# A four-layer mixer trunk on one core: z tiles as the first projections of attention and of gated DeltaNet, a longer lead for them, and the DeltaNet gates as 64 columns

## The chip, the core and the metric

The kernel runs on one core of one Trainium2 chip. The metric is the device time of one execution in microseconds (us). Three executions of the kernel before took 2756.51, 2757.06 and 2751.56 us, with a median of 2756.51. A further execution was recorded by the profiler: it took 2752.67 us, of which the profile's span (first to last instruction) is 2751.0 us, at a mean granted TensorE clock of 0.993. Engines are named as in the profile: PE is TensorE's matmul, PEld its load of the stationary operand, DVE is VectorE, ACT is ScalarE, POOL is GpSimd, SP is SyncE, which starts most transfers.

## The reference

Four layers work on x of 1024 tokens by 1024 features in float32: HGRN2, sliding-window attention (SWA), gated DeltaNet (GDN), HGRN2 again. Each layer does

```
h = rmsnorm(x) * (1 + scale) + shift        # shift, scale, gate come from the condition c (adaLN)
y = mixer(h)                                # ends with  (o * silu(z)) @ w_out
x = x + gate * y
```

What matters here is the combined input projection of the two layers in the middle.

```
# SWA: 16 query heads, 4 key/value heads of 64 features, window 128
q, k, v, z = split(h @ w_in, [1024, 1280, 1536])
q, k = rope(rmsnorm(q)), rope(rmsnorm(k))
o = banded softmax attention with a sink;   y = (o * silu(z)) @ w_out

# GDN: 8 query/key heads, 16 value heads of 128 features
qkv, z, a, b = split(h @ w_in, [4096, 6144, 6160])
q, k, v = split(silu(causal_conv(qkv)));  q, k = l2norm(q), l2norm(k)
beta = sigmoid(b);  g = -exp(a_log) * softplus(a + dt_bias)     # 16 heads each: 32 columns in all
o = gated delta rule over chunks;         y = (rmsnorm(o) * silu(z)) @ w_out
```

## The kernel before

**Precision and tiles.** h is kept transposed (features on the 128 partitions) in two halves of 512 tokens, each as a rounded part and the rest (`hhi[hf]`, `hlo[hf]`). Weights are split in the same way when they are loaded: `load_w` (L158 to L179) transfers 256 KB (`w_raw`), casts it on ACT (`w_hi`, L171) and subtracts on DVE (`w_lo`, L172). There are three buffers of `w_raw` and four each of `w_hi` and `w_lo`. A product takes three matmuls, hi by hi (L196), hi by lo (L197) and lo by hi (L198), all in `mm3`. A tile of `proj_fm` has 128 output features by 512 tokens: 8 steps of K by 3, that is 24 matmuls of 512 moving columns, with two loads of weights for each group of 128 features. A tile of `proj_tm` (SWA's q, k, v) has tokens on the partitions: two blocks of 128 tokens by 256 features, 48 matmuls of 256 columns (`projt_ps`), with four loads of weights for two tiles in a half. All of them draw from three PSUM buffers (`proj_ps`, two in most of the GDN layer), as do the tiles of the output projection (`out_ps`).

**Order.** The program is written in order of emission, and each instruction has a priority from a counter. A scheduler puts the instructions of each engine in a fixed order by these priorities and by what is ready. `high_priority(offset)` takes the given number off the priority of what is emitted inside it. `early(g)` emits the first projections of a layer with `offset=EO`, 60, and the loads of their weights with a further `EW`, 150. `burst()` uses 4000. `weave` mixes several streams of one layer by their stated lengths.

**From layer to layer.** The output projection and the norm run in halves of tokens. Half 0's norm is done while half 1 is still projected. After half 1's last output tile the norm of half 1 is emitted: `norm_stats` (L444 to L468) squares and sums x (L457, L458), gets the row sums by matmuls (`n_ps`, L461), takes an inverse root in small steps on DVE (L151 to L155) and spreads it by a matmul (`n_rb`, L468); `norm_apply` (L471 to L481) writes 8 slices of `n_t` (L479, DVE), `hhi` (L480, ACT) and `hlo` (L481, DVE). Its buffers are a pool that is closed behind it (`self.nst.close()`), and then the next layer opens its own pool and calls `early` with projections of half 0, which need nothing of half 1's norm.

**What early takes.** In SWA it is `kv(0)`: two tiles of k, then two of v. The eviction of k, `ev_k` (L1225 to L1242), is long: sum of squares, inverse root, rotary products (`rotate`, L1215 to L1218), four transposes (`kt_ps`), copies. That of v is one ACT copy (L1247). Behind it come the write of x's half 1 to memory (`spill_x`), `kv(1)`, and `proj(0, ds[0])`: q of group 0 in both halves, then its z. The eviction of z, `ev_z`, is a tanh on ACT (L1267) and one DVE operation (L1270). Then the groups follow, attention of one beside the projections of the next. In GDN it is `proj_kq(0, ds[0], ((0,),))`: one tile of k, one of q and two of z, all of half 0 of head pair 0. k and q go through `conv` (L603 to L619): a copy (L611), a scaled copy (L615), three DVE operations (L617), tanh (L618), a product (L619), over three `gd_tb` and two `gd_xs` buffers, and then transposes (L625). z takes a tanh (L693), one DVE operation (L695) into a single buffer `gd_zs`, and a transfer to memory (`od`). Then come `decays()`, the tiles of k and q of half 1, and the first `inverse` (first matmul `kk_ps`, L714), beside k and q of pair 1 and v and z of pair 0. After that the eight stages run, each with one pair's `scan`, the next pair's `inverse`, and projections as filling; the list `ZL` says which z tiles (pair, halves) fill which stage. In HGRN2 `early` takes q and f of half 0 and the beginning of v.

**decays()** computes the gates a and b (32 columns) for all tokens: for each half one `ab_ps` tile of 24 matmuls with 32 stationary columns (`gd_wab`: hi and lo of the gate weights, cast at L528 and subtracted at L529), a copy to `gd_abT` (L547), eight transposes (`abt_ps`, L550), and then a chain of some 30 small operations up to `d_ps` (L582), on which the first inverse waits.

Of the kernel before, what the change touches and what calls it, by code (L numbers as in the profile page):

```python
# [32 lines left out]
SB = {"q": 2, "tmp": 4, "qhi": 2, "pth": 2, "sm": 2, "zs": 2, "of": 3}  # L33


EO, EW = 60, 150
PRH, PRS, PR = 150, 200, (150, 150)

SPH, SPS = 0.2, 0.4
# [5 lines left out]
ADA_ORDER = (2, 0, 3, 1, 4, 5)  # L45
AO = ((2, True), (0, True), 0, D, (3, True), (1, True))

ZL = ((1, 0, 1), (2, 0, 1)), ((3, 0, 1),), ((4, 0, 1),), ((5, 0),), ((5, 1),), ((6, 0, 1),), ((7, 0, 1),), ()


def drain(g):
    for _ in g:
        pass
# [31 lines left out]
class Trunk:  # L85
# [423 lines left out]
    def gdn(self, i, side):  # L509
# [11 lines left out]
            return gp.tile([P, n], F32, name="gd_" + name, tag="gd_" + name, bufs=bufs)  # L521


        wv = gp.tile([P, 4, KT, 32], F32R, name="gd_wab", tag="blk", bufs=1)
        wab = [wv[:, 0], wv[:, 1]]
        raw = self.wp.tile([P, HT], F32, name="w_raw", tag="raw", bufs=RAW)[:, :KT * 32].rearrange("p (k n) -> p k n", k=KT)
        nc.sync.dma_start(raw, w_in[:, :, 6144:6176])
        nc.scalar.copy(wab[0], raw)  # L528
        nc.vector.tensor_tensor(wab[1], raw, wab[0].bitcast(F32), ALU.subtract)  # L529
        cw = self.taps  # L530

        cmask = gp.tile([P, P], F32, name="gd_cmask")
# [6 lines left out]

        def decays():  # L540
            ab = tl("tmp")
            abT = gp.tile([P, T], F32, name="gd_abT", tag="blk", bufs=1)[:32]
            for hf in range(2):
                ps = self.proj_ps("ab_ps")
                for k in range(KT):
                    self.mm3(ps[:32, :], (wab[0][:, k, :], wab[1][:, k, :]), (self.hhi[hf][:, k, :], self.hlo[hf][:, k, :]), k == 0, k == KT - 1)
                nc.scalar.copy(abT[:, hf * HT:(hf + 1) * HT], ps[:32, :])  # L547
            pt = self.psum("tr", "abt_ps", 1)
            for c in range(C):
                nc.tensor.transpose(pt[:, c * 32:(c + 1) * 32], abT[:, c * P:(c + 1) * P], self.ident[:32, :32])  # L550
            pab = pt[:, :256].rearrange("p (c n) -> p n c", c=C)
            hc = lambda x: x.rearrange("p (h c) -> p h c", h=H)
            par = tl("tmp")
            tri = par[:, P:2 * P]
            nc.gpsimd.memset(tri, 1.0)
            nc.gpsimd.affine_select(out=tri, in_=tri, compare_op=ALU.is_ge, fill=0.0, base=0, pattern=[[1, P]], channel_multiplier=-1)
            nc.sync.dma_start(par[:, 0:16], ins["gd_a_log"].to_broadcast([P, H]))
            nc.sync.dma_start(par[:, 16:32], ins["gd_dt_bias"].to_broadcast([P, H]))
            nc.scalar.activation(par[:, 0:16], par[:, 0:16], AF.Exp)
            nc.scalar.activation(hc(beta), pab[:, 16:32, :], AF.Exp, scale=-1.0)  # L560
            nc.vector.tensor_scalar(beta, beta, 1.0, None, ALU.add)
            nc.vector.reciprocal(beta, beta)
            x, e, s, s2, g = (ab[:, n * P:(n + 1) * P] for n in (0, 1, 2, 3, 0))
            nc.vector.tensor_tensor(hc(x), pab[:, 0:16, :], par[:, 16:32, None].to_broadcast([P, H, C]), ALU.add)

            nc.vector.scalar_tensor_tensor(e, x, -1.0, x, ALU.mult, ALU.max)
            nc.scalar.activation(e, e, AF.Exp, scale=-1.0)
            nc.vector.tensor_scalar(s, e, 2.0, None, ALU.add)
            nc.vector.reciprocal(s, s)
            nc.vector.tensor_tensor(s, s, e, ALU.mult)  # L570
            nc.vector.tensor_tensor(s2, s, s, ALU.mult)
            nc.vector.tensor_scalar(e, s2, 2.0 / 17, 2.0 / 15, ALU.mult, ALU.add)
            for n in (13, 11, 9, 7, 5, 3, 1):
                nc.vector.tensor_tensor(e, e, s2, ALU.mult)
                nc.vector.tensor_scalar(e, e, 2.0 / n, None, ALU.add)
            nc.vector.tensor_tensor(e, e, s, ALU.mult)
            nc.vector.tensor_scalar(x, x, 0.0, None, ALU.max)
            nc.vector.tensor_tensor(e, e, x, ALU.add)
            nc.vector.tensor_scalar(e, e, -1.0, None, ALU.mult)
            nc.vector.tensor_tensor(hc(g), hc(e), par[:, 0:16, None].to_broadcast([P, H, C]), ALU.mult)  # L580
            pd = self.psum("lev", "d_ps", 2)
            nc.tensor.matmul(pd[:, 0:P], tri, g, start=True, stop=True)  # L582
            nc.tensor.matmul(pd[:, P:2 * P], self.ones, g, start=True, stop=True)
            nc.vector.tensor_scalar(nd, pd[:, 0:P], -1.0, None, ALU.mult)
            nc.scalar.activation(ed, pd[:, 0:P], AF.Exp)
            nc.vector.tensor_scalar(ned, ed, -1.0, None, ALU.mult)
            nc.scalar.activation(edl, pd[:, P:2 * P], AF.Exp)
            nc.vector.tensor_tensor(wl, pd[:, P:2 * P], nd, ALU.add)
            nc.scalar.activation(wl, wl, AF.Exp)
            pt = self.psum("tr", "dt_ps", 1)  # L590
            nc.tensor.transpose(pt[:, :P], nd, self.ident)
            dT = tl("tmp")
            nc.vector.tensor_scalar(dT[:, :P], pt[:, :P], -1.0, None, ALU.mult)
            nc.sync.dma_start(ddr.rearrange("h (c t) -> (h c) t", t=P), dT[:, :P])
# [39 lines left out]
        def proj_kq(u, dd, halves=((0, 1),)):  # L634
# [18 lines left out]
            for hv in halves:  # L653
                yield from self.proj_fm(w_in, D + u * P, ev_k, hv)
                yield from self.proj_fm(w_in, u * P, ev_q, hv)
                if hv == (0,):
                    yield from proj_z(u, dd, hv)
                    return
            t8 = lambda name, n=C: gp.tile([P, n], F32, name="gd_" + name, tag=name, bufs=2 if name in ("r2", "gn") else 3)
            ms = dd["ms"]  # L660
# [225 lines left out]

        w_out, od, on = ins["gd_out_w"][0], self.od[1], self.par[:, 74:75]
        ds = [dict() for _ in range(U)]
        self.early(proj_kq(0, ds[0], ((0,),)))
        self.spill_x(1)  # L890
        decays()
        drain(proj_kq(0, ds[0], ((1,),)))
# [282 lines left out]
    def swa(self, i, side):  # L1175
# [70 lines left out]
            p3 = ps.rearrange("p (t n) -> p t n", t=2)  # L1246
            nc.scalar.copy(v[:, v2, :], p3)  # L1247

        def proj(g, d):
            d.update(q=[None, None], zs=[None, None], rq=[None, None])  # L1250

            def ev_q(tp, ps):
                hf = tp // 2
# [7 lines left out]
                    d["rq"][hf] = self.rsqrt(d["ms"], 16, "q", sp)  # L1261

            yield from self.proj_tm(self.load_tm(w_in, g * 256), ev_q)
            for m in range(2):
                def ev_z(hf, ps):
                    th = tl("tmp")
                    nc.scalar.activation(th, ps, AF.Tanh, scale=0.5)  # L1267
                    if m == 0:
                        d["zs"][hf] = tl("zs", n=2 * HT).rearrange("p (m t) -> p m t", m=2)
                    nc.vector.scalar_tensor_tensor(d["zs"][hf][:, m, :], th, 1.0, ps, ALU.add, ALU.mult)  # L1270

                c0 = 1536 + g * 256 + m * P
                yield from self.proj_fm(w_in, c0, ev_z)

        def mix(g, d, halves=(0, 1)):
            vg = v[:, :, g * 64:(g + 1) * 64]
# [68 lines left out]
                yield 1  # L1345

        def kv(hf):
            for c0, ev in ((1024, ev_k), (1280, ev_v)):
                yield from self.proj_tm(self.load_tm(w_in, c0), ev, (2 * hf, 2 * hf + 1))

        self.early(kv(0))
        self.spill_x(1)
        drain(kv(1))
        ds = [dict() for _ in range(G)]
        drain(proj(0, ds[0]))
        w_out, od = ins["sw_out_w"][0], self.od[0]
        for g in range(G - 1):
            weave(self.tc, (mix(g, ds[g]), 28000, 0, 1, PRS), (proj(g + 1, ds[g + 1]), 42000, 0, 1, 0), (take(side, NS[1]), NS[1], 0, 1, 0))
# [89 lines left out]
```

## Time and profile before

| | before |
|---|---|
| median of three runs | 2756.51 us (2751.56 to 2757.06) |
| the profiled execution | 2752.67 us |
| its span | 2751.0 us |
| PE busy | 2669.9 us, 97% |
| DVE busy | 2001.3 us, 73% |
| ACT busy | 1224.1 us, 44% |
| SWA: last output tile of the layer before, first attention work | 632 us, 712 us |
| GDN: last output tile of the layer before, first inverse | 1123 us, 1187 us |
| last HGRN2: last output tile of the layer before | 2175 us |

How to read it: a row of the profile gives line, engine, operation, the tiles it writes and reads, and a count, then busy time and the mean of one in ns, then the time its engine stood idle before it and what ended that. "projt_ps <- DVE w_lo L172: 5.8, 4, 2.9" in a list of waits says that PE, ahead of matmuls into `projt_ps`, stood idle for 5.8 us in all, 4 times, at most 2.9 us, and that DVE's write of `w_lo` ended it. In a timeline the first two columns are start and length in us. In a table of windows the columns are the window, its length, the busy time of PE, PEld, DVE, ACT and POOL with the number of instructions, the granted clock of TensorE (1.00 is full), the mean share of the 16 DMA engines that were busy, and GB/s. Matmuls overlap one another, so their durations don't add up: their pace is read from one start to the next.

### The profile page before, as it was taken

How to read it: one execution, taken by the hardware profiler on the slowest of the kernel's cores; microseconds unless marked ns; L12 is line 12 of the kernel's file. 1: busy time of each engine (PE TensorE's matmuls, PEld its weight loads, DVE VectorE, ACT ScalarE, POOL GpSimd, SP SyncE). 2: the span in 40 equal slices, each digit the busy share in tenths (PEclk: the TensorE clock that was granted, in tenths of full speed). 3: DMA queues.
4: the chain of work that ended last, by engine and by line, in shares of the span. 5: the costliest groups of instructions: out<-in, count | busy, mean ns of one | idle time of the engine just before them, and what ended most of it. 6: DMA issues, size and time to landing. Idle time of an engine off the chain costs nothing.

```text
span 2751.0 us, 51716 instructions
## 1 busy us (share of the span) xinstructions
PE 2669.9 (97%) x19217; PEld 2147.2 (78%) x19217; DVE 2001.3 (73%) x5669; ACT 1224.1 (44%) x3107; POOL 133.8 (5%) x352
## 2 busy tenths in 40 slices
PE   8999999998999999899999999999999999999999
PEld 4878888778878767677788877787778888887877
DVE  6685765778677778677898798988875757556575
ACT  4332333444445565444546455555543433333342
POOL 0000100000000000001101001100000000000000
PEclk9999999999999999999999999999999999999999
DMA  6232222344223243324343343432463211111133
GB/s 237 82 103 82 66 85 74 118 129 146 62 85 97 77 149 91 116 74 111 94 127 101 92 123 101 116 104 77 150 188 119 81 54 40 51 46 49 46 120 112
DMA packets 347666, 273.30 MB, mean 99 GB/s; under 512 B 68963, under 2 KB 276246, under 8 KB 347414
## 3 DMA queue, kind: packets, MB, share of 16 engines
q1 hardware_dynamic: 347126, 268.95, 32.8%
q8 instruction: 151, 2.47, 0.4%
q14 instruction: 101, 0.83, 0.1%
q0 software_dynamic: 288, 1.05, 0.1%
HBM read 224.77 MB, written 45.15 MB: 98 GB/s over the span
## 4 chain that ended last, share of the span: by engine, by line
PE 76%; DVE 11%; DMA 6%; ACT 4%; issue 2%; SPq 1%; POOL 0%; DVEq 0%; ACTq 0%
PE proj_ps L196 10%; PE proj_ps L198 10%; PE proj_ps L197 10%; PE outp_ps L198 4%; PE outp_ps L196 4%; PE outp_ps L197 4%; PE projt_ps L197 3%; PE projt_ps L198 3%; PE projt_ps L196 3%; DMA ada_w<-in_ada_w_dram 2%; PE lev_ps L1004 2%; DVE gd_tb L617 1%; PE pv_ps L1330 1%; DVE w_lo L172 1%; PE w_ps L859 1%
## 5 line engine op out<-in xcount | busy, mean ns | idle before, releaser
L196 PE MATMUL proj_ps<-hhi,w_hi 128*128 128x512 f32 x1664 | 686.1, 412 | 11.2 <-ACT gd_tb L615 8.6
L197 PE MATMUL proj_ps<-hlo,w_hi 128*128 128x512 f32 x1664 | 675.5, 406 | 0.0
L198 PE MATMUL proj_ps<-hhi,w_lo 128*128 128x512 f32 x1664 | 674.0, 405 | 0.0
L196 PEld LDWEIGHTS proj_ps<-hhi,w_hi 128*128 128x128 f32 x1664 | 315.5, 190 | 68.3 <-ACT gd_tb L615 11.0
L198 PEld LDWEIGHTS proj_ps<-hhi,w_lo 128*128 128x128 f32 x1664 | 314.9, 189 | 59.1 <-issue 1.2
L197 PEld LDWEIGHTS proj_ps<-hlo,w_hi 128*128 128x128 f32 x1664 | 315.3, 190 | 53.0 <-issue 1.4
L172 DVE TENSOR_TENSOR w_lo<-w_raw,w_hi 128x512 fp32r<-128x512 f32 x332 | 223.1, 675 | 168.2 <-ACT w_hi L171 165.6
L171 ACT CAST w_hi<-w_raw 128x512 fp32r<-128x512 f32 x332 | 201.9, 611 | 307.8 <-PE proj_ps L197 183.1
L197 PE MATMUL projt_ps<-w_lo,hhi 128*128 128x256 f32 x896 | 256.1, 290 | 5.8 <-DVE w_lo L172 5.8
L196 PE MATMUL projt_ps<-w_hi,hhi 128*128 128x256 f32 x896 | 256.1, 291 | 0.5 <-ACT w_hi L171 0.5
L198 PE MATMUL projt_ps<-w_hi,hlo 128*128 128x256 f32 x896 | 255.4, 290 | 0.0
L196 PE MATMUL outp_ps<-o_hi,w_hi 128*128 128x512 f32 x576 | 229.3, 400 | 2.9 <-ACT o_hi L1156 1.9
L198 PE MATMUL outp_ps<-o_hi,w_lo 128*128 128x512 f32 x576 | 228.0, 398 | 1.4 <-DVE w_lo L175 1.4
L197 PE MATMUL outp_ps<-o_lo,w_hi 128*128 128x512 f32 x576 | 228.8, 398 | 0.2
L197 PEld LDWEIGHTS projt_ps<-w_lo,hhi 128*128 128x128 f32 x896 | 170.7, 192 | 9.2 <-DVE w_lo L172 6.8
L196 PEld LDWEIGHTS projt_ps<-w_hi,hhi 128*128 128x128 f32 x896 | 170.5, 192 | 3.8 <-issue 1.2
L198 PEld LDWEIGHTS projt_ps<-w_hi,hlo 128*128 128x128 f32 x896 | 170.6, 192 | 2.3 <-issue 1.4
L617 DVE SCALAR_TENSOR_TENSOR gd_tb<-gd_xs,taps,gd_tb 128x512 f32<-128x512 f32 x192 | 144.2, 751 | 25.1 <-ACT gd_tb L615 21.5
L174 ACT ACTIVATE w_hi<-w_raw,par 128x512 fp32r<-128x512 f32 (+1 forms) x136 | 94.7, 698 | 142.9 <-PE outp_ps L197 98.8
L196 PEld LDWEIGHTS outp_ps<-o_hi,w_hi 128*128 128x128 f32 x576 | 108.6, 189 | 27.0 <-ACT o_hi L1156 3.9
L175 DVE SCALAR_TENSOR_TENSOR w_lo<-w_raw,par,w_hi 128x512 fp32r<-128x512 f32 (+1 forms) x136 | 96.8, 716 | 42.8 <-ACT w_hi L174 41.5
L198 PEld LDWEIGHTS outp_ps<-o_hi,w_lo 128*128 128x128 f32 x576 | 108.6, 189 | 24.2 <-DVE w_lo L175 1.9
(388 smaller groups left out, 4918.5 us busy)
## 6 DMA issues: line engine op xcount, KB each, us to landing
ada_w<-in_ada_w_dram SPq DMA_DIRECT2D x160, 256.0 KB, 2.8
w_raw<-in_hg_in_w_dram SPq DMA_DIRECT2D x136, 256.0 KB, 2.8
w_raw<-in_gd_in_w_dram SPq DMA_DIRECT2D x108, 256.0 KB, 3.1
o_in<-od SPq DMA_DIRECT2D x72, 256.0 KB, 3.3
w_raw<-in_gd_out_w_dram SPq DMA_DIRECT2D x64, 256.0 KB, 2.8
w_raw<-in_sw_in_w_dram SPq DMA_DIRECT2D x48, 256.0 KB, 3.0
w_raw<-in_hg_out_w_dram SPq DMA_DIRECT2D x40, 256.0 KB, 2.9
ada_w<-in_ada_w_dram SPq DMA_DIRECT2D x8, 1024.0 KB, 10.0
```

Source lines behind the costliest of these rows:

```text
L171: nc.scalar.copy(hi, raw)
L172: nc.vector.tensor_tensor(lo, raw, hi.bitcast(F32), ALU.subtract)
L174: nc.scalar.activation(hi, raw, AF.Copy, scale=scale)
L175: nc.vector.scalar_tensor_tensor(lo, raw, scale, hi.bitcast(F32), ALU.mult, ALU.subtract)
L196: mm(out, a[0], b[0], start=start, stop=False)
L197: mm(out, a[0], b[1], start=False, stop=False)
L198: mm(out, a[1], b[0], start=False, stop=stop)
L617: nc.vector.scalar_tensor_tensor(y, xs[:, j:j + HT], w(j), y, ALU.mult, ALU.add)
L859: nc.tensor.matmul(po[:, hd[a]], dd["u"][a, hf][:, cs], rhs, start=True, stop=True)
L1004: nc.tensor.matmul(pl[gs, c * 48:(c + 1) * 48], kg[:, c * P + g * 32:c * P + (g + 1) * 32], x[:, 4 * c + g, :], start=True, stop=True)
L1330: nc.tensor.matmul(po[a * 64:(a + 1) * 64], vg[:, n + 1 - nkb + b, :], p4[:, :, a, :], start=b == 0, stop=b == nkb - 1)
```

## The change

There are four parts.

1. `EO` goes from 60 to 200, for the `early` block of all four layers.
2. In SWA, `early` takes the two z tiles of half 0 of group 0, then v, then k of half 0. `kv` has v ahead of k in both halves. After `kv(1)` come q (both halves) and z of half 1 alone. The z weights of group 0 are loaded twice, four loads more.
3. In GDN, `early` takes four z tiles of half 0 (pairs 0 and 1), then k and q of half 0 of pair 0. `ZL` has z of pair 1 only for half 1 in the first stage. The z weights of pair 1 are loaded twice, four loads more.
4. In `decays()` the hi and lo weights of the gates stand side by side as 64 stationary columns, so that one matmul makes both products: per half 16 matmuls in place of 24, in a `burst`. The product lo by lo, which the three matmuls leave out, is included. The transposes have 64 columns, and a copy (ACT) and a sum (DVE) of 128x256 put the two parts together.

```diff
-EO, EW = 60, 150
+EO, EW = 200, 150
...
-ZL = ((1, 0, 1), (2, 0, 1)), ((3, 0, 1),), ((4, 0, 1),), ((5, 0),), ((5, 1),), ((6, 0, 1),), ((7, 0, 1),), ()
+ZL = ((1, 1), (2, 0, 1)), ((3, 0, 1),), ((4, 0, 1),), ((5, 0),), ((5, 1),), ((6, 0, 1),), ((7, 0, 1),), ()
...
-        wv = gp.tile([P, 4, KT, 32], F32R, name="gd_wab", tag="blk", bufs=1)
-        wab = [wv[:, 0], wv[:, 1]]
+        wab = gp.tile([P, 2 * KT, 64], F32R, name="gd_wab", tag="blk", bufs=1)[:, :KT, :]
...
-        nc.scalar.copy(wab[0], raw)
-        nc.vector.tensor_tensor(wab[1], raw, wab[0].bitcast(F32), ALU.subtract)
+        nc.scalar.copy(wab[:, :, 0:32], raw)
+        nc.vector.tensor_tensor(wab[:, :, 32:64], raw, wab[:, :, 0:32].bitcast(F32), ALU.subtract)
...
-                ps = self.proj_ps("ab_ps")
-                for k in range(KT):
-                    self.mm3(ps[:32, :], (wab[0][:, k, :], wab[1][:, k, :]), (self.hhi[hf][:, k, :], self.hlo[hf][:, k, :]), k == 0, k == KT - 1)
-                nc.scalar.copy(abT[:, hf * HT:(hf + 1) * HT], ps[:32, :])
+                ps = self.proj_ps("ab_ps")[:64]
+                with self.burst():
+                    for k in range(KT):
+                        nc.tensor.matmul(ps, wab[:, k, :], self.hhi[hf][:, k, :], start=k == 0, stop=False)
+                        nc.tensor.matmul(ps, wab[:, k, :], self.hlo[hf][:, k, :], start=False, stop=k == KT - 1)
+                nc.scalar.copy(abT[:, hf * HT:(hf + 1) * HT], ps)
...
-                nc.tensor.transpose(pt[:, c * 32:(c + 1) * 32], abT[:, c * P:(c + 1) * P], self.ident[:32, :32])
-            pab = pt[:, :256].rearrange("p (c n) -> p n c", c=C)
+                nc.tensor.transpose(pt[:, c * 64:(c + 1) * 64], abT[:, c * P:(c + 1) * P], self.ident[:64, :64])
...
+            p4, ab2 = pt.rearrange("p (c b n) -> p b c n", c=C, b=2), par[:, 2 * P:].rearrange("p (c n) -> p c n", c=C)
+            nc.scalar.copy(ab2, p4[:, 1])
+            nc.vector.tensor_tensor(ab2, ab2, p4[:, 0], ALU.add)
+            pab = ab2.rearrange("p c n -> p n c")
...
                 if hv == (0,):
-                    yield from proj_z(u, dd, hv)
                     return
...
-        self.early(proj_kq(0, ds[0], ((0,),)))
+        self.early(chain(proj_z(0, ds[0], (0,)), proj_z(1, ds[1], (0,)), proj_kq(0, ds[0], ((0,),))))
...
-            for c0, ev in ((1024, ev_k), (1280, ev_v)):
+            for c0, ev in ((1280, ev_v), (1024, ev_k)):
...
-        self.early(kv(0))
+        ds = [dict(q=[None, None], zs=[None, None], rq=[None, None]) for _ in range(G)]
+        self.early(chain(proj_z(0, ds[0], (0,)), kv(0)))
         self.spill_x(1)
         drain(kv(1))
-        ds = [dict() for _ in range(G)]
-        drain(proj(0, ds[0]))
+        drain(chain(proj_q(0, ds[0]), proj_z(0, ds[0], (1,))))
```

`proj_q` and `proj_z` of SWA are the two halves of the former `proj`, which now chains them.

More of the change, by code (lines that the diff above doesn't have):

```diff
@@ L541, in decays @@
             ab = tl("tmp")
-            abT = gp.tile([P, T], F32, name="gd_abT", tag="blk", bufs=1)[:32]
+            abT = gp.tile([P, T], F32, name="gd_abT", tag="blk", bufs=1)[:64]
             for hf in range(2):
-                ps = self.proj_ps("ab_ps")
-                for k in range(KT):
-                    self.mm3(ps[:32, :], (wab[0][:, k, :], wab[1][:, k, :]), (self.hhi[hf][:, k, :], self.hlo[hf][:, k, :]), k == 0, k == KT - 1)
-                nc.scalar.copy(abT[:, hf * HT:(hf + 1) * HT], ps[:32, :])
+                ps = self.proj_ps("ab_ps")[:64]
[4 more added lines that the diff above has]
+                nc.scalar.copy(abT[:, hf * HT:(hf + 1) * HT], ps)
             pt = self.psum("tr", "abt_ps", 1)
             for c in range(C):
-                nc.tensor.transpose(pt[:, c * 32:(c + 1) * 32], abT[:, c * P:(c + 1) * P], self.ident[:32, :32])
-            pab = pt[:, :256].rearrange("p (c n) -> p n c", c=C)
+                nc.tensor.transpose(pt[:, c * 64:(c + 1) * 64], abT[:, c * P:(c + 1) * P], self.ident[:64, :64])
             hc = lambda x: x.rearrange("p (h c) -> p h c", h=H)
             par = tl("tmp")
+            p4, ab2 = pt.rearrange("p (c b n) -> p b c n", c=C, b=2), par[:, 2 * P:].rearrange("p (c n) -> p c n", c=C)
+            nc.scalar.copy(ab2, p4[:, 1])
+            nc.vector.tensor_tensor(ab2, ab2, p4[:, 0], ALU.add)
+            pab = ab2.rearrange("p c n -> p n c")
             tri = par[:, P:2 * P]
@@ L1247, in ev_v, with proj_q @@
             nc.scalar.copy(v[:, v2, :], p3)
-        def proj(g, d):
-            d.update(q=[None, None], zs=[None, None], rq=[None, None])
+        def proj_q(g, d):
             def ev_q(tp, ps):
@@ L1263, in proj, with proj_z @@
             yield from self.proj_tm(self.load_tm(w_in, g * 256), ev_q)
+        def proj_z(g, d, halves=(0, 1)):
             for m in range(2):
@@ L1272, in proj @@
                 c0 = 1536 + g * 256 + m * P
-                yield from self.proj_fm(w_in, c0, ev_z)
+                yield from self.proj_fm(w_in, c0, ev_z, halves)
+        def proj(g, d):
+            return chain(proj_q(g, d), proj_z(g, d))
         def mix(g, d, halves=(0, 1)):
```

## The prediction

> **What bounds the kernel now.** I read the page first, then the waits of PE, then a table of windows at the places that the change touches, then the timeline of PE, ACT and DVE there, and last the tiles of the gate projection.
>
> ```profile
> span 2751.0 us, 51716 instructions
> PE 2669.9 (97%) x19217; PEld 2147.2 (78%) x19217; DVE 2001.3 (73%) x5669; ACT 1224.1 (44%) x3107; POOL 133.8 (5%) x352
> PE   8999999998999999899999999999999999999999
> PE 76%; DVE 11%; DMA 6%; ACT 4%; issue 2%; SPq 1%; POOL 0%; DVEq 0%; ACTq 0%
> ```
>
> The kernel is bound by TensorE: it is busy 2669.9 us of 2751.0, so all its idle time is 81.1 us. A quarter of the chain is other engines, though, and the slices show where to look: of 68.8 us each, only the first, the tenth (619 to 688 us) and the seventeenth (1100 to 1169) fall to 8. Only two things can shorten the time: fewer or cheaper matmuls, or less of those 81 us. Which waits they are, from the waits of PE (in total, times, longest):
>
> ```profile
> PE proj_ps L196 <- ACT gd_tb L615: 8.6, 4, 5.9
> PE projt_ps L197 <- DVE w_lo L172: 5.8, 4, 2.9
> PE ab_ps L196 <- DVE gd_zs L695: 1.3, 1, 1.3
> ```
>
> The first is in the GDN layer, the second in the SWA layer, each right after the projections that run ahead of the norm of half 1. Windows there and in the stages behind (us, busy time of PE, PEld, DVE, ACT, POOL, granted clock, DMA share, GB/s):
>
> ```profile
> 632.00:660.50 28.50, 27.78 (x220) 26.45 (x218) 26.34 (x67) 14.39 (x25) 0.00 (x0) 1.00 0.48 165
> 660.50:666.10 5.60, 1.31 (x10) 0.89 (x8) 3.73 (x7) 2.45 (x4) 0.00 (x0) 0.84 0.67 226
> 666.10:671.00 4.90, 4.85 (x22) 4.86 (x23) 4.43 (x14) 0.26 (x1) 0.00 (x0) 0.50 1.04 369
> 1148.50:1153.30 4.80, 4.65 (x14) 3.38 (x15) 3.39 (x6) 1.61 (x4) 2.06 (x10) 0.59 0.43 109
> 1198.00:1256.00 58.00, 50.16 (x236) 39.64 (x236) 50.22 (x147) 32.51 (x99) 4.25 (x10) 0.99 0.29 75
> 1380.00:1480.00 100.00, 99.90 (x698) 82.10 (x697) 85.64 (x253) 54.39 (x173) 7.81 (x20) 1.00 0.40 110
> 2176.00:2230.00 54.00, 53.73 (x438) 46.63 (x437) 35.21 (x88) 23.23 (x39) 1.53 (x4) 1.00 0.21 60
> ```
>
> In SWA, PE works without a break to 660.5, stands still for most of 5.6 us, and then has only half its clock for 4.9 us, so the stall costs about 2.4 us more than its length. The same happens in GDN after its 5.9 us. The steady GDN stage (1380 on) is at 99.9%, so time saved ahead of it is kept, and so is time lost. The last HGRN2 layer's start has 0.27 us idle in 54: nothing to gain there.
>
> **SWA: tiles of z first, v before k, and a lead of 200.** The cause of the stall stands on DVE's and PE's timelines:
>
> ```profile
> 655.03 0.68 DVE L1215 TENSOR_TENSOR sw_tmp<-projt_ps,sw_sm 128x512 f32<-128x512 f32 x1
> 664.74 0.75 DVE L481 SCALAR_TENSOR_TENSOR hlo<-n_t,mod,hhi 128x512 fp32r<-128x512 f32 x1 [1.87 <-ACT hhi L480]
> 665.41 1.28 DVE L172 TENSOR_TENSOR w_lo<-w_raw,w_hi 128x512 fp32r<-128x512 f32 x2
> ```
> ```profile
> 632.21 0.40 PE L198 MATMUL out_ps<-hg_ohi,w_lo 128*128 128x512 f32 x1
> 632.45 0.28 PE L196 MATMUL projt_ps<-w_hi,hhi 128*128 128x256 f32 x1
> ...
> 658.55 0.28 PE L198 MATMUL projt_ps<-w_hi,hlo 128*128 128x256 f32 x1
> 658.67 0.28 PE L196 MATMUL projt_ps<-w_hi,hhi 128*128 128x256 f32 x1
> 662.26 0.39 PE L197 MATMUL projt_ps<-w_lo,hhi 128*128 128x256 f32 x1 [1.43 <-DVE w_lo L172]
> 666.15 0.58 PE L197 MATMUL projt_ps<-w_lo,hhi 128*128 128x256 f32 x1 [2.91 <-DVE w_lo L172]
> ...
> 1139.72 0.39 PE L196 MATMUL proj_ps<-hhi,w_hi 128*128 128x512 f32 x1
> 1142.21 0.39 PE L198 MATMUL proj_ps<-hhi,w_lo 128*128 128x512 f32 x1
> ```
>
> PE wants the weights of k of half 1, and their low part waits on DVE behind the norm's last write of half 1. DVE had been busy 26.34 of 28.5 us with the norm, the weights and k's rotary eviction (L1215 is one of its operations) at once. How much of DVE that eviction took up to the norm's end, by its tiles sw_tmp and k_ms (windows of those alone), and what a load of weights and an eviction of z take there:
>
> ```profile
> 632.00:665.50 33.50, 1.20 (x8) 0.79 (x8) 4.94 (x8) 1.18 (x2) 0.98 0.50 171
> ```
> ```profile
> 632.00:665.50 33.50, 2.56 (x10) 0.98 0.50 171
> ```
> ```profile
> L172 DVE TENSOR_TENSOR w_lo<-w_raw,w_hi 128x512 fp32r<-128x512 f32 x332 | 223.1, 675 | 168.2 <-ACT w_hi L171 165.6
> ```
> ```profile
> L1270 DVE SCALAR_TENSOR_TENSOR sw_zs<-sw_tmp,proj_ps x16: 657/680/689, 732.3 to 996.1; 128x512 f32<-128x512 f32 x16
> ```
>
> The work on half 0 that needs no norm grows. A projt matmul starts 0.12 us after the last (658.55, 658.67), so the four tiles of 48 are 23 us of PE; the 5 us that are left to 660.5 are norm matmuls and transposes. A full matmul of 512 takes 0.226 us from start to start (twelve from 1139.72 to 1142.21, in GDN), so two z tiles of 24 add 10.9. So this work lasts from 632.45 to about 671. On DVE, k's eviction leaves the norm's stretch: 4.94 + 2.56, less the two reductions of some 0.68 that write k_ms from sw_tmp and stand in both, 6.1 us. In come four loads of weights and two evictions of z: 4 x 0.675 + 2 x 0.68 = 4.1. The norm's last write then lies some 2 us ahead of 664.7, about 8 us before PE needs what stands behind it. The two long stalls go (1.43 + 2.91 = 4.3 us) and with them the half clock (2.4): -6.8 rounded. Best, all four waits of that row go: 5.8 + 2.4 = -8.2. Worst, DVE stays the bound and pays the added loads in the same stretch: 4 x 0.675 = +2.7. I take -6.8, as 8 us of margin are more than those 2.7.
>
> The four added transfers go where DMA stands at 0.48, so at nothing; without that cover they would come out as the +2.7 does, a late w_lo. Tiles of z are only moved: q and z of half 1 follow as before. The lead of 200 puts casts and evictions further ahead of the norm's instructions, but gives no tile of PSUM earlier: the first projt (632.45) starts after the last out tile's matmul (632.21), and I expect the same of z.
>
> **GDN: the gate weights as 64 columns.**
>
> ```profile
> 1155.70 0.42 PE L196 MATMUL ab_ps<-hhi,gd_wab 128*32 128x512 f32 x1
> 1161.06 0.40 PE L198 MATMUL ab_ps<-hhi,gd_wab 128*32 128x512 f32 x1
> ...
> 1186.78 0.83 PE L714 MATMUL kk_ps<-gd_k 128*128 128x128 f32 x6
> ```
> ```profile
> L196 PE MATMUL ab_ps<-hhi,gd_wab x16: 391/396/423, 1155.7 to 1169.3; 128*32 128x512 f32 x16
> L550 PE MATMUL abt_ps<-ident,gd_abT x8: 220/222/243, 1171.0 to 1172.0; 32*128 32x32 f32 x8
> ```
> ```profile
> 1148.38 0.40 ACT L528 CAST gd_wab<-w_raw 128x256 fp32r<-128x256 f32 x1
> ```
>
> Full matmuls start 0.226 us apart, as above; twenty-four with 32 columns go from 1155.70 to 1161.06, 5.36/23 = 0.233 each. So the number of stationary columns doesn't set the pace, and 64 columns cost what 32 do. 48 matmuls become 32: 16 x 0.233 = -3.7 us. The bounds are -3.6 (0.226) and, if 64 columns cost twice 32, 32 x 0.466 - 48 x 0.233 = +3.7; I take -3.7, since 32 and 128 columns differ by 3%. The eight transposes become 64 wide, still short (0.22 us each). The copy and the sum of the two halves add two operations of 128x256; the wab cast of that size took 0.40, so 0.8 us, in a chain from 1171 to the first inverse at 1186.78; PE has the tiles of k and q of half 1 as cover there (11 us), so nothing; 0.8 us if it doesn't.
>
> A rule of the Trainium skill speaks against this part: TensorEngine Tiling (Array Packing), in its Overview, has up to 4 tiles side by side for 32 columns and up to 2 for 64. By it 48 matmuls in fours would be an estimated 2.8 us and 32 in pairs 3.7, a loss of 0.9. The trace doesn't bear it out: with 0.233 us between starts nothing runs side by side here.
>
> **GDN: the order of the early tiles.** PE and ACT around the stall:
>
> ```profile
> 1148.54 0.80 PE L196 MATMUL proj_ps<-hhi,w_hi 128*128 128x512 f32 x1 [5.94 <-ACT gd_tb L615]
> ```
> ```profile
> 1146.04 1.38 ACT L480 ACTIVATE hhi<-n_t,mod 128x512 fp32r<-128x512 f32 x2 [1.11 <-DVE n_t L479]
> 1147.33 0.57 ACT L611 COPY gd_xs<-proj_ps 128x512 f32<-128x512 f32 x1
> ```
>
> Three tiles fill PE's three PSUM buffers before the norm ends, and the first to be emptied, k's, is copied only after ACT's last hhi, though its matmuls were long done; the wab cast (1148.38) comes after that too. In SWA evictions passed the norm (655.03 before 664.74); here none did, with the same lead of 60. So I read it as a dependence on the norm's end (this layer's pool opens when the norm's is closed), not as a place in a queue: three other tiles and a lead of 200 will stop at the same point, and the 5.94 us and its half clock stay. Behind the stall the order is now z, gates, k and q of half 1; it becomes z, k, q, gates, k and q of half 1. Two tiles more (2 x 24 x 0.226 = 10.9), the gates 3.7 shorter, and the wait of 1.3 behind the gates' first half gone, since z's eviction of one operation on each engine no longer stands behind a convolution: the first inverse starts 10.9 - 3.7 - 1.3 = 5.9 us later, at about 1192.7. Two z tiles are then missing from the first stage (-10.9). Net beside the gates -1.3, if that stage is limited by PE; its second load of z weights is 4 x 0.675 us of DVE in a span where DVE is 73% busy, so nothing.
>
> **Layers 0 and 3** change by the lead alone. With 0.27 us idle in 54 nothing is to be had. A loss is bounded by SWA's stall, 6.8, if an eviction now holds up the norm; I take +1 as a bare allowance for layer 3, near the idle end, and 0 for layer 0.
>
> **Sum** against the profiled run's own time of 2752.67 (span and 1.67 around it): -6.8 - 3.7 - 1.3 + 1 = -10.8, so 2741.9. The median of the three runs shown is 3.84 above the profiled run, so 2745.7, given as 2746. About 0.2% (5.5 us) is what a measurement of this kernel can tell from no change.
>
> **The rivals.** (1) *SWA's stall is only replaced.* The low weights of v of half 1 can stand behind the norm's last writes as those of k did; DMA at 1.04 in 666 to 671 speaks for it, the 8 us of margin against. Then SWA gives 0: -4.0, 2752.5, no change that shows. Chance 0.17.
>
> (2) *The first GDN stage is not limited by PE.* In 1198 to 1256 PE has 7.8 us idle. If the later start of the inverse isn't made up by the missing z tiles, they leave holes: +5.9 (the gates' gain in it) in place of -5.0, altogether +0.1, 2756.6, no change. Chance 0.08.
>
> (3) *Slower: the convolutions become the bound.* k and q of half 0 are computed behind two z tiles, so their convolutions begin at about 1160.5 rather than 1147.3, and DVE, 50.22 of 58 us busy in 1198 to 1256 and level with PE there, has all of them still to do. If its queue never catches up, the whole 13.2 us appear at the inverse and in the stage behind, with the z tiles' PE time lost as holes: +13.2 in place of -5.0, so +7.4 in all, 2763.9. It decides when the first kk_ps starts later than about 1199 on this trace's clock. Against it: DVE has 27% free over the run, and loses nothing but the order. Chance 0.13.
>
> (4) *The lead does in GDN what I deny*: evictions pass the norm, and 5.94 and 2.0 (half of 4.8 at clock 0.59) go: -18.7, 2737.8. Chance 0.09. The reverse, that the lead moves nothing anywhere, is nearly my forecast: there the order of tiles and the 64 columns do the work.
>
> **How the numbers follow.** My forecast has 0.53, so faster 0.53 + 0.09 = 0.62, same 0.17 + 0.08 = 0.25, slower 0.13. The range takes in (4) at its low end and (1) and (2) at its high end: 2737 to 2758; (3) is left out. The forecast's own range, with SWA from -8.2 to -3.9 (the stall of 2.91 stays) and layer 3 from 0 to +3, is 2743 to 2751.
>
> **What would show it.** In the SWA layer: no stall on w_lo between 655 and 672 and granted clock 1.00 there; the last hlo before about 664. In GDN: ab_ps x32 in all, in some 7.5 us; a stall of about 6 us before the fourth tile; kk_ps first at about 1193 less SWA's 7, 1186; PE at 97% or more from there. It is wrong if w_lo waits show up elsewhere in SWA with the same sum, if kk_ps starts past 1192 on that clock, or if layer 3's start has idle time.

## The result, and the profile after

The changed kernel took 2778.28 us in the median of six runs (2773.44 to 2783.98), the kernel before 2754.09 in six runs (2750.77 to 2764.03). The ratio is 1.008, with a 95% interval from 1.006 to 1.0101: slower by 0.8%, where 0.4% less had been forecast, and outside the range. The profiled execution of the changed kernel took 2782.53 us, its span 2780.7.

The page of the changed kernel, the rows that answer to those of before:

```profile
span 2780.7 us, 51771 instructions
PE 2677.7 (96%) x19201; PEld 2156.8 (78%) x19201; DVE 1999.5 (72%) x5678; ACT 1229.3 (44%) x3116; POOL 134.1 (5%) x352
PE   8999999999999999789999999999999999999999
PE 78%; DVE 10%; DMA 5%; ACT 4%; issue 2%; SPq 1%; DVEq 0%; ACTq 0%
```

Sixteen matmuls are gone, and the sum of PE's busy time still grew by 8 us: part of its matmuls ran at a lower clock (0.987 in the mean of the profiled execution, 0.993 before). Idle time of PE grew from 81 to 103 us. The slice at the start of GDN, the seventeenth, went from 8 to 7, and the one behind it from 9 to 8; that of SWA, the tenth, from 8 to 9. The waits of PE in the changed kernel (in total, times, longest; lines from the GDN layer on have moved down by 4 or 5):

```profile
PE proj_ps L196 <- DVE gd_zs L699: 16.9, 2, 14.1
PE proj_ps L196 <- ACT gd_tb L620: 10.2, 9, 3.8
PE n_rb L468 <- DVE n_sq L466: 3.0, 1, 3.0
PE projt_ps L197 <- DVE w_lo L172: 3.0, 4, 1.8
PE projt_ps L196 <- ACT hhi L480: 2.8, 4, 0.9
```

SWA's waits for `w_lo` did shrink, from 5.8 to 3.0. But the one stall in GDN grew from 5.9 to 14.1 us, and matmuls now wait for `hhi` itself, that is for the norm, which no row of before showed. Windows of the changed kernel around these places (the columns as before):

```profile
637.30:673.90 36.60, 36.60 (x253) 33.65 (x251) 24.56 (x49) 16.41 (x28) 0.00 (x0) 1.00 0.46 154
673.90:676.00 2.10, 0.35 (x5) 0.14 (x3) 2.10 (x5) 1.65 (x3) 0.00 (x0) 1.00 0.00 0
676.00:681.00 5.00, 4.39 (x20) 4.09 (x21) 4.92 (x13) 1.19 (x3) 0.00 (x0) 0.54 0.51 157
1151.30:1165.40 14.10, 0.05 (x1) 0.00 (x0) 12.81 (x19) 6.99 (x12) 0.00 (x0) 0.50 0.15 38
1165.40:1170.00 4.60, 4.57 (x11) 3.60 (x12) 1.11 (x2) 0.47 (x3) 0.00 (x0) 0.50 0.61 176
2196.00:2248.00 52.00, 48.39 (x410) 41.57 (x409) 33.51 (x84) 20.80 (x34) 1.57 (x4) 1.00 0.13 39
```

In SWA, DVE is no longer full while PE works on half 0 (24.56 of 36.6 us, where it was 26.34 of 28.5): most of k's eviction has left, as forecast. PE stands still at the end of it all the same. In the last HGRN2 layer, where nothing but the lead changed, the start has 3.6 us idle in 52.

**Where the time went, by layer.** The first matmul into `n_rb` of half 0 of each layer marks a point that the early tiles don't touch; between these marks the span falls into four parts. All kernels of this study stand in the table (E8, where the marks themselves were moved, only by its span; the parts are differences of marks that were rounded to 0.1 us). The last two columns are for the whole span: the time in which PE stood idle, and an estimate of what a low clock cost, which is half of PE's busy time in the stretches where the profile has a granted clock of 0.50.

| kernel | up to SWA | SWA | GDN | last HGRN2 | span | PE idle | half clock |
|---|---|---|---|---|---|---|---|
| before | 589.0 | 475.1 | 1072.3 | 614.6 | 2751.0 | 81.1 | 15.3 |
| changed | 594.5 | 475.0 | 1092.1 | 619.1 | 2780.7 | 103.0 | 27.9 |
| E1 changed, lead 60 | 590.1 | 469.3 | 1086.1 | 616.5 | 2762.0 | 90.8 | 19.7 |
| E2 before, lead 200 | 593.7 | 476.4 | 1089.9 | 619.6 | 2779.6 | 94.4 | 33.0 |
| E3 before, 64 columns | 590.9 | 475.1 | 1071.5 | 614.8 | 2752.3 | 81.1 | 22.0 |
| E4 changed, statistics first | 593.0 | 473.9 | 1080.8 | 617.1 | 2764.8 | 94.8 | 16.7 |
| E5 SWA's order, 64 columns, lead 60 | 589.6 | 470.6 | 1068.1 | 615.1 | 2743.4 | 75.2 | 16.5 |
| E6 before, GDN's order | 591.6 | 473.0 | 1086.8 | 615.9 | 2767.3 | 87.4 | 24.9 |
| E7 as E1, abt_ps in other buffers | 591.4 | 469.9 | 1073.6 | 616.2 | 2751.1 | 80.7 | 17.4 |
| E8 changed, exit of half 1 first | | | | | 2760.3 | 90.1 | 18.1 |
| E9 as E5, lead 0 | 593.5 | 469.5 | 1068.7 | 614.8 | 2746.5 | 77.1 | 20.7 |
| E10 as E5, z of pair 0 first | 589.5 | 471.2 | 1069.0 | 615.0 | 2744.7 | 72.1 | 22.0 |
| E11 as E5, lead 200 in SWA | 591.3 | 475.8 | 1069.1 | 614.8 | 2751.0 | 81.0 | 19.7 |
| E12 as E5, lead 200 in GDN | 593.0 | 469.4 | 1074.7 | 614.9 | 2752.0 | 86.2 | 11.6 |

Kernels that share the code of a part differ in it by up to 4 us in the first part (before, E5, E12) and 2 in SWA (before, E3, E6), so smaller differences are not read. Of the changed kernel's 29.7 us, 19.8 lie in GDN, 5.5 ahead of SWA, 4.5 in the last layer and none in SWA, where a gain had been forecast.

By the last two columns, 21.9 us of the 29.7 are idle time and 12.6 the clock, while PE's own work shrank. The clock is no fixed cost of a kernel. Of the 23 executions of the kernel before that were taken beside E9 and E10, the shortest, 2746.41 us, had a mean clock of 0.995, and the longest, 2770.54 us, one of 0.987. The six of the changed kernel have 0.986 to 0.990. So a difference of some us between two profiled executions can be the clock alone, and the parts of the table are read together with the medians.

### The profile page after: what moved, and what is told of

Same layout as the page of the kernel before. It is cut to its first block, busy times and chain, and to the rows that moved or that the text cites. A ratio compares the mean times of both kernels' runs of the same rounds, so it can differ in the third digit from the quotient of the medians.

```text
span 2780.7 us, 51771 instructions
## 1 busy us (share of the span) xinstructions
PE 2677.7 (96%) x19201; PEld 2156.8 (78%) x19201; DVE 1999.5 (72%) x5678; ACT 1229.3 (44%) x3116; POOL 134.1 (5%) x352
## 4 chain that ended last, share of the span: by engine, by line
PE 78%; DVE 10%; DMA 5%; ACT 4%; issue 2%; SPq 1%; DVEq 0%; ACTq 0%
PE proj_ps L196 11%; PE proj_ps L198 11%; PE proj_ps L197 11%; PE outp_ps L198 4%; PE outp_ps L196 4%; PE outp_ps L197 4%; PE projt_ps L197 3%; PE projt_ps L196 3%; PE projt_ps L198 3%; PE lev_ps L1008 2%; DMA ada_w<-in_ada_w_dram 2%; PE pv_ps L1338 1%; PE o_ps L1081 1%; PE pt_ps L1332 1%; PE o_ps L1082 1%
## 5 line engine op out<-in xcount | busy, mean ns | idle before, releaser
L196 PEld LDWEIGHTS projt_ps<-w_hi,hhi 128*128 128x128 f32 x896 | 173.0, 194 | 12.6 <-ACT hhi L480 3.6
```

What stands on the lines that cost most here:

```text
L196: mm(out, a[0], b[0], start=start, stop=False)
```

## The experiments

Two theories came first. **A:** the lead of 200 does the harm. PE's instructions stand in the one order that the scheduler gave them; the early tiles now stand ahead of the few matmuls of the norm and of the last output tile, so the norm comes late, and all that waits for the norm. **B:** the new order does it, since k and q of GDN come behind four z tiles.

What A rests on is the timeline of PE at the start of GDN, first before and then in the changed kernel, and that of ACT at the norm's end in the changed kernel:

```profile
1112.38 0.39 PE L196 MATMUL out_ps<-sw_of,w_hi 128*128 128x512 f32 x1
...
1123.04 0.39 PE L198 MATMUL out_ps<-sw_of,w_lo 128*128 128x512 f32 x1
...
1128.99 1.05 PE L461 MATMUL n_ps<-ones,n_acc 128*128 128x1 f32 x8 [0.35 <-DVE n_acc L458]
...
1133.09 1.10 PE L468 MATMUL n_rb<-n_sq,ones 128*128 128x512 f32 x2 [0.20 <-DVE n_sq L466]
```
```profile
1127.42 0.39 PE L196 MATMUL proj_ps<-hhi,w_hi 128*128 128x512 f32 x1
...
1138.10 0.39 PE L198 MATMUL proj_ps<-hhi,w_lo 128*128 128x512 f32 x1
1138.33 0.39 PE L197 MATMUL out_ps<-sw_of,w_hi 128*128 128x512 f32 x1
...
1146.08 0.95 PE L461 MATMUL n_ps<-ones,n_acc 128*128 128x1 f32 x8
1150.07 1.28 PE L468 MATMUL n_rb<-n_sq,ones 128*128 128x512 f32 x2 [3.04 <-DVE n_sq L466]
...
1165.43 0.80 PE L196 MATMUL proj_ps<-hhi,w_hi 128*128 128x512 f32 x1 [14.09 <-DVE gd_zs L699]
```
```profile
1163.28 0.72 ACT L480 ACTIVATE hhi<-n_t,mod 128x512 fp32r<-128x512 f32 x1 [1.48 <-DVE n_t L479]
1163.90 1.55 ACT L697 ACTIVATE gd_tb<-proj_ps 128x512 f32<-128x512 f32 x3
```

Two z tiles (1127.42 to 1138.10) run ahead of the last matmuls of the last output tile (1138.33), a third ahead of the norm's sums (`n_ps`, 1146.08). The norm needs both, so `n_rb` is 32 us behind the start of that output projection (1117.67) where it was 21 behind (1112.4 to 1133.1). No eviction of GDN goes before the norm's end: ACT takes the three z tiles right behind its last `hhi` (1163.90). The three PSUM buffers are full by 1146, so PE has nothing left to do, and it waits 14.09 us.

**E1: the changed kernel with the lead at 60.**

```diff
-EO, EW = 200, 150
+EO, EW = 60, 150
```

> The changed kernel with the lead of the early blocks back at 60; the new order of tiles and the 64 columns stay. Theory A (the lead does the harm: early matmuls stand ahead of the norm's few matmuls and the last output tile on TensorE's in-order queue, so the norm of half 1 comes late): n_rb returns to about 649, 1133 and 2183 us and the time falls to 2740 to 2752. Theory B (the order does the harm: k and q of DeltaNet behind four z tiles delay the convolutions and the first inverse): the time stays within 8 us of the changed kernel, 2770 to 2786, and kk_ps starts after 1200 still.

Measured: 2761.89 us, ratio to before 1.002 [1.0006, 1.0033]. 16.4 us of the loss went, `n_rb` is back (646, 1128 and 2192 us), and SWA takes 5.8 us less than before. But the kernel is still slower than before by 5.7 us in the median, all of it and more in GDN (+13.8), where the first `kk_ps` starts at 1205.9. So A holds for the larger part and misses its own number; B has a part too.

**E2: the kernel before with the lead of 200.**

```diff
-EO, EW = 60, 150
+EO, EW = 200, 150
```

> The kernel before with nothing but the lead of 200. Theory A: most of the loss is here, 2768 to 2785, with n_rb late in all layers (by some 10 us in each of attention, DeltaNet and the last HGRN2 layer). Theory B: no change, 2750 to 2758.

Measured: 2778.12 us, 1.0075 [1.005, 1.01]. The lead alone costs as much as the whole change. B's forecast for this run falls.

**E3: the 64 columns alone.** The edit is the change's hunks on `gd_wab` and in `decays()`, and nothing else of it.

> The kernel before with nothing but the gate weights as 64 columns (and their burst). Both theories: 32 matmuls of ab_ps at 0.23 us, 3.7 us less TensorE work, so 2748 to 2753. If 64 columns cost twice 32, or the added copy and sum hold up the first inverse, 2755 to 2760.

Measured: 2754.28 us, 0.9991 [0.9974, 1.0008]: between no change and the 3.7 us forecast, not told apart. The mean clock of its ten executions was 0.9905, that of the 27 of the kernel before 0.9919, so a part of a gain may be hidden by the clock; no run shows it. The pace of the 64 columns is, in the timeline of E7, which has them as well (the first and the last of sixteen):

```profile
1166.22 0.45 PE L547 MATMUL ab_ps<-hhi,gd_wab 128*64 128x512 f32 x1
...
1169.73 0.39 PE L548 MATMUL ab_ps<-hlo,gd_wab 128*64 128x512 f32 x1
```

3.51/15 = 0.234 us from start to start, against 0.233 with 32 columns.

**E4: the changed kernel with the statistics of half 1's norm in a burst.**

```diff
-        self.norm_apply(i, hf, self.norm_stats(hf))
+        with self.burst() if hf else ExitStack():
+            rb = self.norm_stats(hf)
+        self.norm_apply(i, hf, rb)
```

> The changed kernel, in which the statistics of half 1's norm (squares, sums, the inverse root, n_ps and n_rb) are emitted in a burst, so that the early tiles don't pass them; what writes hhi and hlo stays where it was. Theory A: the norm starts again right after the last output tile, half or more of the loss goes: 2750 to 2768. Theory B: within 6 us of the changed kernel.

Measured: 2768.31 us, 1.0043 [1.0025, 1.0061]. Ten of the 16.4 us that the lead costs come back, for a matter of ten matmuls and some small operations that get priority over the early tiles. In GDN `n_ps` now starts at 1138.7, but the last output tile still ends there (last start 1136.0), behind the z tiles.

**E8: output projection and statistics of half 1 both with the lead of the early tiles.**

```diff
-            drain(t)
+            with tc.high_priority(offset=EO) if hf and nxt is not None else ExitStack():
+                drain(t)
...
-        self.norm_apply(i, hf, self.norm_stats(hf))
+        with self.tc.high_priority(offset=EO) if hf else ExitStack():
+            rb = self.norm_stats(hf)
+        self.norm_apply(i, hf, rb)
```

> The changed kernel with its lead of 200, but the output projection of half 1 and the statistics of its norm get the same lead, so that early tiles pass neither. Theory A (the lead hurts because early tiles stand ahead of the last output tile and of the norm's matmuls): n_ps follows the last output tile at once, the time is that of the order at a lead of 60, 2758 to 2766. Rival (what hurts is the place of the early evictions and casts on VectorE and ScalarE): 2766 to 2780, near the run where the statistics alone went first.

Measured: 2765.96 us, 1.0036 [1.002, 1.0052], at the upper edge of what A gives and not clear of E4. `n_ps` follows the last output tile in GDN (1126.7, 1129.4). The edit also moved the output projection into the work ahead of it, so this run bears A out only weakly. E4 and E8 stay 6.4 and 4.1 us above E1, so the place of the early loads, casts and evictions on the other engines may have a part of the lead's loss; no run takes that apart.

For the loss that E1 left, the next two pairs were set against one another. **C:** it lies in GDN's order, and SWA's part is worth what was forecast. **F:** within GDN, the gates' chain waits in a PSUM buffer that it shares with the transposes of k and q; **G:** the convolutions of k and q are the bound themselves.

**E5: SWA's order and the 64 columns, lead 60, GDN's early tiles as before.** The edit is the change without its first line, the line of `ZL` and the two hunks on `proj_kq`.

> Attention's new order of tiles and the 64 columns, at the lead of 60; DeltaNet's early tiles as before. Theory C (at a lead of 60 the loss of the changed order is all in DeltaNet, and attention's part is worth what was forecast, 5 to 7 us): 2746 to 2752, with the output tiles ahead of DeltaNet some 6 us earlier than before. Theory D (attention's gain is taken back behind it): 2753 to 2758.

Measured: 2747.4 us, 0.9978 [0.9961, 0.9995]: faster than both kernels. SWA takes 4.5 us less. Its waits of `projt_ps` for `w_lo`, four and 5.8 us in all before, are one of 0.2 us; two for `w_hi` in SWA, 1.5 us together, stay.

**E6: GDN's order alone.**

```diff
-ZL = ((1, 0, 1), (2, 0, 1)), ((3, 0, 1),), ((4, 0, 1),), ((5, 0),), ((5, 1),), ((6, 0, 1),), ((7, 0, 1),), ()
+ZL = ((1, 1), (2, 0, 1)), ((3, 0, 1),), ((4, 0, 1),), ((5, 0),), ((5, 1),), ((6, 0, 1),), ((7, 0, 1),), ()
...
                 if hv == (0,):
-                    yield from proj_z(u, dd, hv)
                     return
...
-        self.early(proj_kq(0, ds[0], ((0,),)))
+        self.early(chain(proj_z(0, ds[0], (0,)), proj_z(1, ds[1], (0,)), proj_kq(0, ds[0], ((0,),))))
```

> The kernel before with nothing but DeltaNet's new early order (z of two pairs, then k and q of half 0), at the lead of 60 and with 32 gate columns. Theory C: the order alone costs 10 to 18 us, 2766 to 2774, and the first kk_ps starts at 1200 or later. Rival E (the burst of the 64-column gates, which puts them ahead of q's tile, is what delays the inverse): 2754 to 2760.

Measured: 2768.36 us, 1.0032 [1.0017, 1.0047], GDN +14.5 us, the first `kk_ps` at 1207.5. The order alone does it, without the burst: C holds for GDN, and rival E falls. By the estimate of the last column, 10.6 of the 14.5 us in this profile are the clock and 4.2 are idle time; in the medians E6 is 11.9 us above before.

**E7: the gates' transposes in other buffers.** The tag "tr" has one PSUM buffer, and its tiles are handed out in the order of the program: `ktr_ps`, `qtr_ps`, then `abt_ps`. In the new order k and q of half 0 are late, and with them the gates. E1's timeline of PE shows it:

```profile
1189.55 0.60 PE L630 MATMUL qtr_ps<-ident,gd_q 128*128 128x128 f32 x4
1192.09 0.71 PE L552 MATMUL abt_ps<-ident,gd_abT 64*128 64x64 f32 x8
1204.90 0.77 PE L587 MATMUL d_ps<-gd_tmp 128*128 128x128 f32 x2 [7.12 <-DVE gd_tmp L585]
1205.46 0.63 PE L588 MATMUL d_ps<-gd_tmp,ones 128*128 128x128 f32 x2
1205.88 0.42 PE L718 MATMUL kk_ps<-gd_k 128*128 128x128 f32 x1
```
```profile
1168.06 1.06 ACT L549 COPY gd_abT<-ab_ps 64x512 f32<-64x512 f32 x2 [0.82 <-PE ab_ps L548]
```

The gates lay ready in `gd_abT` at 1169.1 (the second fence, ACT), but their transposes come at 1192.09, behind those of q, and PE then waits 7.12 us for the chain that hangs on them. The edit:

```diff
-            pt = self.psum("tr", "abt_ps", 1)
+            pt = self.psum("lev", "abt_ps", 2)
```

> The changed kernel at the lead of 60, with one edit: the tile of the gates' transposes, abt_ps, comes from the PSUM buffers of d_ps and not from the single one which it shares with the transposes of k and q. Theory F (the gates' chain waits in that one buffer behind q's convolution, and the first inverse waits for the chain): abt_ps moves from 1192 to about 1170, d_ps no longer waits 7 us, the first kk_ps starts 5 to 12 us earlier, 2750 to 2757. Rival G (the convolutions of k and q are the bound themselves): abt_ps earlier, but the time stays at 2758 to 2765.

Measured: 2752.68 us, 0.9985 [0.9972, 0.9999], 9.2 us less than E1 for one tag. In E7's timeline:

```profile
1170.99 0.46 PE L552 MATMUL abt_ps<-ident,gd_abT 64*128 64x64 f32 x4
1171.82 0.46 PE L552 MATMUL abt_ps<-ident,gd_abT 64*128 64x64 f32 x4
1184.08 0.46 PE L587 MATMUL d_ps<-gd_tmp 128*128 128x128 f32 x2 [0.25 <-DVE gd_tmp L585]
1184.38 0.39 PE L588 MATMUL d_ps<-gd_tmp,ones 128*128 128x128 f32 x2
1184.60 1.06 PE L718 MATMUL kk_ps<-gd_k 128*128 128x128 f32 x8
```

The transposes come 21 us earlier, and the first inverse with them; GDN takes 12.5 us less than in E1. F holds, G falls for the larger part. What went is idle time of PE in GDN, 11.6 us. The first `kk_ps` now stands 123.3 us behind the mark, 122.7 before. GDN is still 5.5 us longer than in E5, where k and q come first: 2.1 of it are idle time and some 2.6 the clock. The first `kk_ps` of the other half starts at 1209.0, so the later convolutions may be the reason for the idle part, but no run takes that apart.

**E9: E5 with no lead at all.**

```diff
-EO, EW = 60, 150
+EO, EW = 0, 150
```

> As the run with attention's new order and the 64 columns (2747.4), with the lead of the early blocks cut from 60 to 0. Theory A (a lead costs as soon as early tiles pass the norm's matmuls; at 60 they pass none that matters): 2743 to 2752, no change from that run. If a lead of 60 still costs something, 2738 to 2743; if early tiles need a lead to fill TensorE beside the norm, 2752 or more, with idle time behind the last output tile of attention and DeltaNet.

Measured: 2745.78 us, 0.9965 [0.9947, 0.9983]: E5 again.

**E10: E5 with z of pair 0 ahead of k and q.** The edit is E7's and, in GDN,

```diff
                 if hv == (0,):
-                    yield from proj_z(u, dd, hv)
                     return
...
-        self.early(proj_kq(0, ds[0], ((0,),)))
+        self.early(chain(proj_z(0, ds[0], (0,)), proj_kq(0, ds[0], ((0,),))))
```

> As the run with attention's new order and the 64 columns (2747.4), but DeltaNet's early tiles are z of pair 0 (two tiles), then k and q, with the gates' transposes in the PSUM buffers of d_ps. Half of the change's order, then, with no tile of pair 1. Theory F (with the shared buffer out of the way the order costs what the later convolutions of k and q cost, some 5 us for four z tiles): 2747 to 2752. If only the shared buffer mattered: 2742 to 2747.

Measured: 2746.06 us, 0.9958 [0.9938, 0.9979], not told apart from E5 and E9. It lies in the range given for the shared buffer alone and 0.9 us below that of F, too little to decide; two z tiles ahead of k and q cost nothing that shows, and win nothing: the stall behind the norm is there as before (6.5 us).

**E11 and E12: E5 with the lead of 200 in one layer.** `early` gets the lead as an argument, and one call passes 200: SWA's in E11, GDN's in E12.

```diff
-    def early(self, g):
+    def early(self, g, lead=EO):
...
-        with self.tc.high_priority(offset=EO):
+        with self.tc.high_priority(offset=lead):
```

> As the run with attention's new order and the 64 columns (2747.4), with the lead of 200 in attention's early block alone. Theory A: v's and z's tiles pass the norm's matmuls, n_rb comes some 8 us later after the last output tile than at 60, and attention loses the 5 to 6 us that its order won: 2751 to 2756. If the lead does no harm there: 2744 to 2750.

Measured: 2752.0 us, 0.9986 [0.9965, 1.0008]. SWA takes 475.8 us and not 470.6: its gain is gone, and 5 us is what A gave. In E11 `n_ps` begins 19 us behind the last output matmul, at a lead of 60 (E5) 9 us.

> The same with the lead of 200 in DeltaNet's early block alone (k, q and z of pair 0, as before). Theory A, from the run of the kernel before with that lead in all layers, where DeltaNet took 17 us longer: 2760 to 2768, the last output tile behind two early tiles, n_ps behind three, and a stall of PE of 10 us or more in place of 5.9. If the loss needs the changed order as well: 2744 to 2752.

Measured: 2756.05 us, 1.0012 [0.9995, 1.0029], 8.6 us above E5 where 13 to 21 had been expected; GDN takes 6.6 us longer. The mechanism is that of the changed kernel, with k and q in place of z; E12's PE:

```profile
1131.66 0.39 PE L197 MATMUL out_ps<-sw_of,w_hi 128*128 128x512 f32 x1
...
1139.45 0.95 PE L461 MATMUL n_ps<-ones,n_acc 128*128 128x1 f32 x8
1143.44 2.05 PE L468 MATMUL n_rb<-n_sq,ones 128*128 128x512 f32 x2 [3.04 <-DVE n_sq L466]
1158.15 0.79 PE L196 MATMUL proj_ps<-hhi,w_hi 128*128 128x512 f32 x1 [12.66 <-ACT gd_tb L620]
```

The stall of 12.66 us stands where E5 has 6.0. In E2 the lead cost GDN 17.6 us, with 32 columns and no burst; the first `kk_ps` comes equally late in both (132.5 us behind the mark, 122.7 before). The other 11 us of E2 are spread over the later stages, and the windows from the first `kk_ps` to the next mark, of E2 and then of E12, say what they are:

```profile
1202.50:2160.00 957.50, 936.33 (x6076) 757.47 (x6075) 771.03 (x2131) 493.52 (x1448) 66.13 (x160) 0.98 0.39 112
1194.90:2137.10 942.20, 920.51 (x6075) 744.43 (x6073) 771.28 (x2131) 493.12 (x1448) 65.27 (x160) 1.00 0.40 114
```

The idle time is the same, 21.2 and 21.7 us, and so is the number of matmuls; the difference of 15.8 us in PE's busy time goes with the granted clock, 0.98 against 1.00. E12's profiled execution was a lucky one in this: its clock was 0.993, the mean of its ten executions 0.990.

## Why the prediction was wrong, point by point

**The step that failed first** is the one on the lead: it "gives no tile of PSUM earlier", so that "other tiles and a lead of 200 will stop at the same point". In SWA the first half held: the first early matmul starts right behind the last output matmul (637.31, 637.55). In GDN it did not: tiles took PSUM ahead of the last output tile's end. And in both layers the step counted only what the early tiles wait for. It did not ask who waits behind them on PE's queue: `n_ps` and `n_rb`, ten short matmuls on which all of the norm hangs. In GDN this turned the 5.94 us, which I let stand, into 14.09. E12 (GDN), E11 (SWA), E4 (those matmuls put back) show it; 16.4 us of the 24 are the lead (changed against E1). In the profiled executions of these two, 18.7 us apart, 12.2 of that is idle time and 8.2 the clock by the estimate of the table. The forecast counted the half clock behind the stalls it had named and none elsewhere.

**That no eviction of GDN passes the norm's end** was right (ACT, 1163.28 and 1163.90), and it is why the earlier tiles win nothing in GDN: they weren't emptied earlier, they only filled the buffers sooner. Rival (4) falls.

**SWA: -6.8 forecast.** The order alone gave -5.8 (E1) and -4.5 (E5), so the mechanism and nearly the size were right: PE's idle time in SWA fell by 4.3 us in both, as much as the two stalls that were to go, and the clock gave 2.5 in E1 and 0.8 in E5, for 2.4 forecast. The lead took it back (E11, changed kernel: 0). "8 us of margin" was reckoned from a norm that starts as before; with `n_rb` at 662.3 it was used up, and a wait of 1.75 us for `w_lo` and its half clock (0.54 for 5 us) stood there again.

**GDN's order: -1.3 forecast, some +14 measured** (E1 with the gates, E6 without). The two tiles' work did go from the first stage as reckoned: in E1 the first `kk_ps` comes 23.8 us later than before, counted from the mark, and the layer 13.8, so 10.0 are recovered, for 10.9 forecast; this is a net figure, in which the clock took some 5.5 back, so the agreement is in part luck. What failed is the start of the inverse, 5.9 us later by the forecast. It was summed along PE's tiles. The gates' transposes were taken to follow the gates' matmuls, since in the trace of before they do; that they also follow q's transposes in one buffer, which k's and q's early place had hidden, was not looked for. Rival (3) had the sign, the place (a `kk_ps` later than 1199) and nearly the sum, but another mechanism: what made the inverse late was for the larger part the shared buffer (E7), not DVE. The +14 themselves hold some 5 (E1) and 11 us (E6) that are the clock by the estimate, which the forecast of this part did not have.

**The 64 columns: -3.7 forecast.** The pace is as forecast, 0.234 us; the gain in time is not shown by E3 alone (-0.8 in GDN, ratio interval on both sides of 1). The Trainium skill's rule (TensorEngine Tiling (Array Packing), Overview), by which 64 columns would have been the worse choice, is borne out by no run here: neither 32 nor 64 columns ran side by side.

**Layers 0 and 3: +1 forecast.** In the last layer the lead cost 4.5 to 5 us (changed, E2), inside the bound of 6.8 and well above the +1 taken. `n_rb` of half 1 comes at 2228.0 us, 66 us behind that of half 0, where it was 46. For the first layer 5.5 and 4.7 us in the table stand against a spread of 4 between kernels with the same code, and E9 has 4.5 with no lead. By the estimate the clock accounts for 3.2, 3.4 and 5.1 of these three, so what the lead itself costs there, 1 to 2 us, is not settled.

## What to carry to other kernels

Moving work earlier in an engine's order is only free if nothing short and urgent stands where it is put: look on each queue for the few instructions behind the moved block on which a whole chain hangs, and give those the priority, not the bulk. Where the consumers of early work can't run before a certain point, more or earlier early work only fills the buffers sooner. And when the order of producers changes, go through every single-buffered tag that they share with others: whoever comes next in program order inherits the delay of the one before.

## What was not expected of the hardware

The half clock came behind a short wait, and also behind no wait at all. In the changed kernel PE has 0.35 us of work in the 2.1 us up to 676.0, with one wait of 1.75 us, and its granted clock was 0.54 from 676 to 681. The Trainium skill (TensorE: Matmul & The Clock Gate, Part 1) gives one idle window of some 3.4 us as what sets the clock back; here less stood ahead of it. In a later stage of GDN, in the same profile, nothing did:

```profile
1380.00:1400.00 20.00, 19.98 (x246) 15.76 (x245) 19.38 (x61) 10.55 (x31) 5.46 (x12) 1.00 0.52 130
1400.00:1413.70 13.70, 13.70 (x103) 11.93 (x92) 6.38 (x11) 6.57 (x17) 1.07 (x3) 0.50 0.17 46
```

PE was busy in all of the 20 us up to 1400.0 and then had half its clock for 13.7 us. Much of that work is short matmuls, and such stretches come in every stage; E12 has them too, and its clock is 1.00 in the mean of all its later stages (the window above). So what sets the clock back isn't only a stall, and what else does is not shown by any run here.
